# Dense products of a two-sequence encoder layer: token parts of 512 and 272 (256) columns in place of two equal halves

## The chip, the cores and the metric

The kernel runs on one core of one Trainium2 chip. The metric is the device time of one execution in microseconds, and the time of a kernel is the median of its runs. TensorE (PE) multiplies, VectorE (DVE), ScalarE (ACT) and GpSimd (POOL) work on vectors, and SyncE (SP) issues the DMAs. All of them run their own instruction streams in order and meet at semaphores.

## The reference

Two sequences, of 512 and of 256 tokens with 1024 features, each get the same 16 meta tokens in front and pass through one layer. All values are float32.

```python
h = h + 0.5 * swiglu(rmsnorm(h, ffn1_norm_w), ffn1_w_gate, ffn1_w_up, ffn1_w_down)   # width 2816
u = rmsnorm(h, mix_norm_w)
q, k, v, z, xbc, dt_raw = split(u @ w_in)                                            # 1024 -> 5408
att = diff_attention(q, k, v, rel_bias, ...)            # 8 heads, two softmaxes each
ssm = ssd_mixer(z, xbc, dt_raw, ...)                    # convolution, state space both ways, gate, norm
h = h + concatenate([att, ssm]) @ w_out                 # 2048 -> 1024
h = h + 0.5 * swiglu(rmsnorm(h, ffn2_norm_w), ffn2_w_gate, ffn2_w_up, ffn2_w_down)
return rmsnorm(h, final_norm_w)[:, 16:]
```

The meta tokens are the same for both sequences, so up to the mixer they are computed once.

## The kernel before

Features lie on the 128 partitions and tokens along the columns. The first feed-forward and the input projection work on T1 = 784 columns (16 meta, 512, 256), the output projection and the second feed-forward on T2 = 768. A dense product (`dense`, `mm3`) takes each float32 operand as a large part and a rest, and makes three matmuls for each 128 rows of the inner dimension: L246, L247 and L248, with a weight block of 128 x 128 as the stationary and a range of token columns as the moving operand. One unit is all the matmuls of one 128-row output block over one part of the tokens: 24 for an inner dimension of 1024, 12 or 6 in the products that are done in pieces (`down`, `o_unit`). A unit goes to one bank of PSUM (`ps_mm` and `ps_x`, two buffers each, 512 columns wide), and one VectorE or ScalarE operation takes it from there.

The parts of the tokens are in two lists: HALF1 (two times 392 of T1) and HALF2 (two times 384 of T2). REAL is HALF2 moved by the 16 meta columns, for the products z and q. HALF1 is used by the first feed-forward, by `x_unit` (the state-space mixer's input), `dt_unit` and `k_units` (keys). HALF2 is used by `o_unit` (output projection) and the second feed-forward. Two places have other parts: the first feed-forward's first gate and up products take PARTS (272, 256, 256), and the second's last down product takes LAST (512, 256).

`ffn` goes through pairs of feature blocks, gate then up, and adds the down product up in six groups. In the last group it goes over all eight output blocks for the first part of the tokens, then over all for the second. `Norm.after` follows it there: for each output block it squares the sum on ScalarE (L294) and adds the squares up on GpSimd (L295), with VectorE for the last block (L298). When the eighth block of a part is done, `Norm.chain` is put on the agenda: `tok_rstd` sums the squares by token on TensorE (L306) and takes 1/sqrt in a dozen small VectorE operations, `diags` and `bcast` (L275, L283, L285) spread it over the partitions, and `make_u` makes the eight normed row blocks, each with L317 on VectorE, L147 on ScalarE and L148 on VectorE. A column of `tok_rstd` holds the token count `tn`: 98 for HALF1, 128 for HALF2. `done`, called after each unit, takes the next weights apart (L147, L148 on 1024 columns) and moves each entry of the agenda one step on. So the norm of the first part goes on beside the products of the second. The same class stands between the output projection and the second feed-forward, there behind the last of the four parts of `o_unit`.

Beside the input projection the state-space mixer goes on as a row of side steps, some for each unit (PACE). Beside attention, units of k, v and the output projection are handed out by the list FILL, a number for each tile of queries. The order on each engine is that of the program with small shifts by the framework's planner, which orders by its own estimates.

Of the kernel before, what the change touches and what calls it, by code (L numbers as in the profile page):

```python
# [47 lines left out]
def body(tc, x_prompt, x_sample, meta_tokens, ffn1_norm_w, ffn1_w_gate, ffn1_w_up, ffn1_w_down,  # L48
# [48 lines left out]
    # Silu's table, before the first data are there  # L97
# [3 lines left out]
    HALF1 = [(0, T1 // 2), (T1 // 2, T1 // 2)]  # L101
    HALF2 = [(0, T2 // 2), (T2 // 2, T2 // 2)]
# [47 lines left out]
    @contextmanager  # L150
    def behind(ins):
        """Keep the engines' order: first ins, then what is in the block."""
        with ExitStack() as st:
            for i in ins:
                st.enter_context(tc.issue_after(i.ins))
            yield
# [66 lines left out]
    def done(free=0):  # L223
        """A dense product has been issued: the next weights, then a step of what goes on beside it."""
# [6 lines left out]
    def complete(gen):  # L231
        """All of gen is issued by now."""
        if gen in agenda:
            agenda.remove(gen)
            for _ in gen:
                pass
# [21 lines left out]
    def rsqrt(v, name):  # L258
        """1/sqrt of a small tile of positive numbers: a first guess from the bits, then Newton's steps."""
# [11 lines left out]
    def diags(r, tiles):  # L271
        """diag(r[:n, j]) for each of tiles (j, n)."""
# [5 lines left out]
    def bcast(dst, dg, tiles):  # L278
        """dst's columns get the diagonals of dg, the same on each partition."""
# [7 lines left out]
    def add_sq(h, m, sums):  # L287
        """The squares of row m; the last row's are added to the others' sum by tok_rstd."""
# [11 lines left out]
    def tok_rstd(sums, n, tn, name):  # L300
        """sums of [P, n]: squares by feature row; 1/rms per token, tn tokens to a column."""
# [10 lines left out]
    def make_u(h, w, r_bc, c0, c1, u, ks):  # L312
        """u = the normed rows, columns c0..c1, split; r_bc starts at c0."""
# [9 lines left out]
    class Norm:  # L323
        """Follows the last additions to h, one half of the tokens at a time."""

        def __init__(self, h, w, halves, tn, name):
            self.__dict__.update(h=h, w=w, halves=halves, tn=tn, name=name)
# [4 lines left out]
        def after(self, m, hf):  # L332
            o, n = self.halves[hf]
            add_sq(self.h[m][:, o:o + n], m, self.ss.setdefault(hf, []))
            if m == KD - 1:
                self.chains[hf] = self.chain(o, n, self.ss[hf])
                later(self.chains[hf])

        def get(self, hf):
            """The split rows, good for a half (or, without one, whole)."""  # L340
# [4 lines left out]
        def chain(self, o, n, ss):  # L345
# [3 lines left out]
            tiles = [(j, self.tn) for j in range(n // self.tn)]  # L349
            r = tok_rstd(ss, n, self.tn, self.name)  # L350
# [9 lines left out]
    def ffn(f, h, halves, u, after, first=None, last=None, rms=None):  # L360
        """first, last: other parts of the tokens for the first gates and the last sums; rms: 1/rms, if u is without."""
# [106 lines left out]
    # the first norm's 1/rms, which the products with the gates get afterwards  # L468
# [9 lines left out]
    def put_h(eng, j, ps, c, n):  # L478
        """One engine to a tile of PSUM."""
# [8 lines left out]
    def squares(tiles):  # L488
        """Sums of squares by token; the squares themselves go nowhere."""
# [8 lines left out]
    def first_norm(tiles, ss):  # L498
        """1/rms of some of the tokens."""
# [9 lines left out]
    def take_x(b, ins):  # L509
        """Two tiles of tokens; ins: what their work on each engine stays behind."""  # L510
# [25 lines left out]
    # the first two tiles one by one, the meta tokens with the first  # L536
# [59 lines left out]
    def parameters():  # L596
# [31 lines left out]
        # the relative bias as a function of the distance, one row per head  # L628
# [22 lines left out]
    nm = Norm(h1, mixw, HALF1, 98, "nm")  # L651
# [32 lines left out]
    HT = T1 // 2  # L684
# [3 lines left out]
    def dt_unit(ws):  # L688
        """Both parts of w against the large part of u, side by side; they are added up in the transposes."""
# [12 lines left out]
    def x_unit(ws, t, hf, free):  # L702
# [12 lines left out]
        else:  # L715
            S.copy(pad[:, 3 + HT:3 + HT + E0], ps[:, :E0])
            S.copy(pad[:, SO + 3 + NMETA:SO + 3 + NMETA + NSA], ps[:, E0:HT])
# [656 lines left out]
```

## Time and profile before

| | us |
|---|---|
| median of 3 runs | 1912.74 |
| lowest, highest | 1911.93, 1917.85 |
| span of the profiled execution, first to last instruction | 1908.7 |
| TensorE busy | 1865.3 (98%) |
| VectorE busy | 1012.4 (53%) |
| ScalarE busy | 699.2 (37%) |
| GpSimd busy | 97.0 (5%) |

The profiled execution's own time stands in the profile only as its span; what a timed run has above a span (start and end) is in the runs' figures alone. A matmul's printed duration contains the way through the array, which overlaps with the next one, so the time that a matmul takes from TensorE's stream is the distance between two starts. The granted clock (PEclk) is a share of full speed, 1.00 being 2.4 GHz and 0.50 being 1.2 GHz.

### The profile page before, as it was taken

The page shows a single profiled execution, that of the slowest core. Times are in us where ns is not written, and L with a number is a line of the kernel's source. Part 1 is how long each engine was busy: PE and PEld are TensorE (multiplying, and loading weights), DVE is VectorE, ACT ScalarE, POOL GpSimd, SP SyncE. Part 2 cuts the span into 40 slices and gives each one's busy share as a digit, 9 for nine tenths or more (in the row PEclk, how much of TensorE's full clock was granted, in tenths as well). Part 3 has the DMA queues.
Part 4 walks back from the last instruction along what each step waited for, and adds up shares of the span by engine and source line. Part 5 has one row for each costly group of instructions (what it writes and reads, how often), then busy time and mean ns, then how long its engine had stood idle before and what let it go on. Part 6 is the DMA issues. An engine that isn't in the chain of part 4 may idle for free.

```text
span 1908.7 us, 27592 instructions
## 1 busy us (share of the span) xinstructions
PE 1865.3 (98%) x11174; PEld 1798.8 (94%) x11174; DVE 1012.4 (53%) x2025; ACT 699.2 (37%) x1410; POOL 97.0 (5%) x118
## 2 busy tenths in 40 slices
PE   8999999999999999999899999999999999999998
PEld 7999999999998997888898998999999999999997
DVE  6444343344437498667788787666542424232333
ACT  6222121212123353678467675433322121222224
POOL 0000000000012000224100000002000000000002
PEclk9999999999998999999999999999899999999999
DMA  4242221222112232888432225321121212122111
GB/s 136 61 165 69 65 66 46 66 67 67 57 54 92 69 85 77 228 219 210 147 94 83 73 82 195 104 78 45 56 78 59 63 56 77 56 67 67 58 53 67
DMA packets 161266, 169.77 MB, mean 89 GB/s; under 512 B 9921, under 2 KB 146234, under 8 KB 161138
## 3 DMA queue, kind: packets, MB, share of 16 engines
q1 hardware_dynamic: 161122, 168.00, 28.7%
q8 instruction: 88, 1.44, 0.3%
q14 instruction: 40, 0.33, 0.1%
q10 hardware_dynamic: 16, 0.00, 0.0%
HBM read 148.54 MB, written 22.87 MB: 90 GB/s over the span
## 4 chain that ended last, share of the span: by engine, by line
PE 86%; DVE 7%; ACT 3%; DMA 1%; issue 1%; POOL 0%; SPq 0%; POOLq 0%; DVEq 0%; ACTq 0%
PE ps_mm L248 15%; PE ps_mm L247 15%; PE ps_mm L246 15%; PE ps_x L246 11%; PE ps_x L248 11%; PE ps_x L247 11%; DVE w L726 2%; PE ps_s L1162 2%; PE ps_s L1280 1%; DMA w<-ar_d 1%; ACT w L909 1%; DVE wl L148 1%; PE ps_s L841 1%; DVE w L1072 1%; DVE w L1182 1%
## 5 line engine op out<-in xcount | busy, mean ns | idle before, releaser
L248 PE MATMUL ps_mm<-rowu,wh 128*128 128x384 f32 (+3 forms) x1408 | 477.1, 339 | 4.8 <-DVE rowu L148 4.6
L246 PE MATMUL ps_mm<-rowu,wh 128*128 128x384 f32 (+3 forms) x1408 | 476.7, 339 | 4.6 <-DVE w L1041 2.0
L247 PE MATMUL ps_mm<-rowu,wl 128*128 128x384 f32 (+3 forms) x1408 | 475.9, 338 | 1.0 <-DVE wl L148 1.0
L148 DVE TENSOR_TENSOR wl<-wr,wh 128x1024 fp32r<-128x1024 f32 (+1 forms) x194 | 234.4, 1209 | 258.2 <-ACT wh L147 257.8
L147 ACT CAST wh<-wr 128x1024 fp32r<-128x1024 f32 (+1 forms) x194 | 198.4, 1024 | 391.0 <-PE ps_x L248 358.0
L247 PE MATMUL ps_x<-rowu,wl 128*128 128x392 f32 (+3 forms) x832 | 282.0, 339 | 0.0
L246 PE MATMUL ps_x<-rowu,wh 128*128 128x392 f32 (+3 forms) x832 | 281.9, 339 | 0.0
L248 PE MATMUL ps_x<-rowu,wh 128*128 128x392 f32 (+3 forms) x832 | 281.8, 339 | 0.0
L246 PEld LDWEIGHTS ps_mm<-rowu,wh 128*128 128x128 f32 x1408 | 266.0, 189 | 10.1 <-issue 2.7
L248 PEld LDWEIGHTS ps_mm<-rowu,wh 128*128 128x128 f32 x1408 | 265.6, 189 | 8.8 <-DVE rowu L148 6.4
L247 PEld LDWEIGHTS ps_mm<-rowu,wl 128*128 128x128 f32 x1408 | 265.9, 189 | 3.1 <-issue 1.4
L246 PEld LDWEIGHTS ps_x<-rowu,wh 128*128 128x128 f32 x832 | 158.5, 190 | 0.1
L247 PEld LDWEIGHTS ps_x<-rowu,wl 128*128 128x128 f32 x832 | 158.4, 190 | 0.0
L248 PEld LDWEIGHTS ps_x<-rowu,wh 128*128 128x128 f32 x832 | 158.1, 190 | 0.0
L147 ACT CAST w<-w 128x384 fp32r<-128x384 f32 (+4 forms) x106 | 59.0, 557 | 231.6 <-DVE w L390 228.5
L246 PE MATMUL ps_x<-w,wh 128*128 128x392 f32 (+3 forms) x352 | 119.7, 340 | 0.0
L246 PE MATMUL ps_mm<-w,wh 128*128 128x392 f32 (+3 forms) x352 | 119.5, 339 | 0.0
L248 PE MATMUL ps_mm<-w,wh 128*128 128x392 f32 (+3 forms) x352 | 119.4, 339 | 0.0
L248 PE MATMUL ps_x<-w,wh 128*128 128x392 f32 (+3 forms) x352 | 119.3, 339 | 0.0
L247 PE MATMUL ps_x<-w,wl 128*128 128x392 f32 (+3 forms) x352 | 119.0, 338 | 0.0
L247 PE MATMUL ps_mm<-w,wl 128*128 128x392 f32 (+3 forms) x352 | 118.8, 338 | 0.0
L410 DVE SCALAR_TENSOR_TENSOR w<-ps_x,w 128x392 f32<-128x392 f32 (+3 forms) x96 | 53.8, 561 | 113.1 <-PE ps_x L248 113.1
(286 smaller groups left out, 2587.8 us busy)
## 6 DMA issues: line engine op xcount, KB each, us to landing
wr<-in_ffn_w_gate_dram SPq DMA_DIRECT2D x44, 512.0 KB
wr<-in_ffn_w_up_dram SPq DMA_DIRECT2D x42, 512.0 KB
wr<-in_w_in_dram SPq DMA_DIRECT2D x42, 512.0 KB
wr<-in_ffn_w_down_dram SPq DMA_DIRECT2D x40, 512.0 KB
w<-ar_d SPq DMA_DIRECT2D x24, 512.0 KB
wr<-in_w_out_dram SPq DMA_DIRECT2D x16, 512.0 KB
w<-ar_d SPq DMA_DIRECT2D x24, 256.0 KB
w<-q_d SPq DMA_DIRECT2D x32, 192.0 KB
```

The lines of the kernel that those rows point to most:

```text
L147: a = S.copy(hi, src)
L148: return a, V.tensor_tensor(lo, src, hi.bitcast(F32), ALU.subtract)
L246: nc.tensor.matmul(ps, ah, bh, start=start, stop=False)
L247: nc.tensor.matmul(ps, al, bh, start=False, stop=False)
L248: last_mm[0] = nc.tensor.matmul(ps, ah, bl, start=False, stop=stop)
L410: V.scalar_tensor_tensor(dst, ps[:, :n], 0.5, dst, ALU.mult, ALU.add)
L726: V.scalar_tensor_tensor(acc, pad[:, j:j + XW], prmT[:, cw:cw + 1], acc, ALU.mult, ALU.add)
L841: nc.tensor.matmul(ps[64 * d:64 * d + 64, g, :], B[:n, 64 * g:64 * g + 64], xd[:n, g * 512:(g + 1) * 512], start=True, stop=True)
L909: S.activation(ab[d][:, h, :], ab[d][:, h, :], AF.Exp, bias=ssm["asp"][:, c, col_s:col_s + 1])
L1072: V.tensor_tensor(dst[b], ps[a, s0:s1], dst[a].bitcast(F32), ALU.subtract)
L1162: nc.tensor.matmul(ps[:, b, :w], qh[c][part][:, P * i:P * i + P], kh[c][:, k0 + b * w:k0 + b * w + w], start=part == 0, stop=part == 1)
L1182: V.tensor_tensor_reduce(out=e[:, :nk].rearrange("p (b w) -> p b w", b=nb), in0=pss[c][:, :nb, :w], in1=tb[:, x0:x0 + nk].rearrange("p (b ...
```

## The change

HALF1 becomes 512 and 272 columns, HALF2 (and with it REAL) 512 and 256. The norm's token count per column becomes one for each part: 128 and 68 for HALF1 (four columns each), 128 and 128 for HALF2 (four columns and two). The small tiles of `tok_rstd` get a name of their own for each part. In `x_unit` the boundary between the two sequences, at column 528, falls 16 columns into the second part, so the copies of the first part are of 512 and 16 columns and those of the second of 16 and 256. The comments are taken out.

```diff
-    HALF1 = [(0, T1 // 2), (T1 // 2, T1 // 2)]
-    HALF2 = [(0, T2 // 2), (T2 // 2, T2 // 2)]
+    HALF1 = [(0, 512), (512, T1 - 512)]
+    HALF2 = [(0, 512), (512, T2 - 512)]
...
-        def __init__(self, h, w, halves, tn, name):
-            self.__dict__.update(h=h, w=w, halves=halves, tn=tn, name=name)
+        def __init__(self, h, w, halves, tns, name):
+            self.__dict__.update(h=h, w=w, halves=halves, tns=tns, name=name)
...
-                self.chains[hf] = self.chain(o, n, self.ss[hf])
+                self.chains[hf] = self.chain(o, n, self.tns[hf], self.ss[hf])
...
-        def chain(self, o, n, ss):
+        def chain(self, o, n, tn, ss):
...
-            tiles = [(j, self.tn) for j in range(n // self.tn)]
-            r = tok_rstd(ss, n, self.tn, self.name)
+            tiles = [(j, tn) for j in range(n // tn)]
+            r = tok_rstd(ss, n, tn, self.name + str(o))
...
-    nm = Norm(h1, mixw, HALF1, 98, "nm")
+    nm = Norm(h1, mixw, HALF1, (128, 68), "nm")
...
-    HT = T1 // 2
+    HT = 512
...
-            S.copy(pad[:, SO + 3 + NMETA:SO + 3 + NMETA + NSA], ps[:, E0:HT])
+            S.copy(pad[:, SO + 3 + NMETA:SO + 3 + NMETA + NSA], ps[:, E0:n])
...
-    nf = Norm([None] * KD, n2w, HALF2, P, "nf")
+    nf = Norm([None] * KD, n2w, HALF2, (P, P), "nf")
```

## Rows read from the trace of the kernel before

**Rows 1.** The page's head and its first part: busy us, share, instructions.

```profile
span 1908.7 us, 27592 instructions
PE 1865.3 (98%) x11174; PEld 1798.8 (94%) x11174; DVE 1012.4 (53%) x2025; ACT 699.2 (37%) x1410; POOL 97.0 (5%) x118
```

**Rows 2.** Who waited for whom, TensorE, whole span: us, times, longest.

```profile
PE ps_x L922 <- DVE w L914: 5.4, 6, 2.2
PE ps_mm L248 <- DVE rowu L148: 4.6, 4, 1.7
PE ps_x L306 <- POOL w L295: 3.0, 2, 2.5
```

**Rows 3.** Stretches: us, PE, PEld, DVE, ACT, POOL busy (count), PEclk, DMA.

```profile
572.10:591.70 19.60, 19.60 (x121) 19.31 (x121) 16.68 (x37) 8.50 (x15) 5.63 (x4) 1.00 0.39 135
591.70:600.30 8.60, 4.73 (x26) 4.14 (x24) 8.60 (x11) 3.85 (x9) 4.06 (x4) 0.98 0.48 173
600.30:611.50 11.20, 11.18 (x49) 11.13 (x49) 3.16 (x17) 0.56 (x2) 1.89 (x17) 0.56 0.08 21
...
1312.50:1331.50 19.00, 18.98 (x117) 18.70 (x116) 16.20 (x36) 7.86 (x13) 5.38 (x4) 1.00 0.19 56
1331.50:1339.90 8.40, 5.70 (x26) 4.58 (x26) 8.40 (x11) 3.70 (x8) 3.34 (x3) 0.84 0.20 64
1339.90:1349.50 9.60, 9.60 (x43) 9.60 (x42) 3.16 (x16) 2.15 (x3) 0.00 (x0) 0.60 0.19 56
...
1000.00:1100.00 100.00, 98.38 (x672) 90.08 (x670) 82.19 (x269) 69.36 (x195) 0.00 (x0) 1.00 0.24 74
```

**Rows 4.** Groups by form, TensorE, L248: count | busy us, mean ns.

```profile
L248 PE MATMUL ps_mm<-rowu,wh 128*128 128x384 f32 x832 | 282.9, 340 | 3.4 <-DVE rowu L148 3.2
...
L248 PE MATMUL ps_mm<-rowu,wh 128*128 128x392 f32 x528 | 179.6, 340 | 1.4 <-DVE rowu L148 1.4
...
L248 PE MATMUL ps_mm<-w,wh 128*128 128x392 f32 x176 | 60.0, 341 | 0.0
...
L248 PE MATMUL ps_x<-w,wh 128*128 128x384 f32 x144 | 48.6, 337 | 0.0
```

**Rows 5.** Instructions in order of time, TensorE, starts of units: start us, us.

```profile
24.70 0.29 PE L246 MATMUL ps_mm<-rowu,wh 128*128 128x272 f32 x1
...
30.73 0.28 PE L246 MATMUL ps_mm<-rowu,wh 128*128 128x256 f32 x1
...
323.67 0.34 PE L246 MATMUL ps_mm<-rowu,wh 128*128 128x392 f32 x1
...
332.24 0.34 PE L246 MATMUL ps_mm<-rowu,wh 128*128 128x392 f32 x1
...
1353.77 0.33 PE L246 MATMUL ps_x<-rowu,wh 128*128 128x384 f32 x1
...
1362.09 0.33 PE L246 MATMUL ps_x<-rowu,wh 128*128 128x384 f32 x1
...
1864.72 0.39 PE L246 MATMUL ps_mm<-w,wh 128*128 128x512 f32 x1
...
1881.20 0.28 PE L246 MATMUL ps_mm<-w,wh 128*128 128x256 f32 x1
...
1884.05 0.28 PE L246 MATMUL ps_mm<-w,wh 128*128 128x256 f32 x1
```

**Rows 6.** Groups by form, VectorE and GpSimd, at 392, 512 and 256 columns.

```profile
L410 DVE SCALAR_TENSOR_TENSOR w<-ps_x,w 128x392 f32<-128x392 f32 x48 | 27.1, 565 | 54.3 <-PE ps_x L248 54.3
...
L410 DVE SCALAR_TENSOR_TENSOR w<-ps_x,w 128x512 f32<-128x512 f32 x4 | 2.8, 692 | 7.8 <-PE ps_x L248 7.8
...
L410 DVE SCALAR_TENSOR_TENSOR w<-ps_x,w 128x256 f32<-128x256 f32 x4 | 1.7, 425 | 3.9 <-PE ps_x L248 3.9
...
L295 POOL TENSOR_TENSOR w<-w,w 128x392 f32<-128x392 f32 x12 | 15.4, 1284 | 64.5 <-ACT w L294 64.5
...
L295 POOL TENSOR_TENSOR w<-w,w 128x256 f32<-128x256 f32 x6 | 4.4, 734 | 12.6 <-ACT w L294 12.6
```

## The prediction

> **What bounds the kernel now.** I read the page's head first. TensorE is busy for 1865.3 of 1908.7 us [rows 1], so a reader should look for two things: what one matmul costs in TensorE's own stream, and the few places where TensorE waits. The waits of TensorE [rows 2] are short, and two kinds matter here. One is for rows of the normed input (L148, written by VectorE) and for the sums of squares (L295 on GpSimd, ahead of L306). The other is the state-space mixer's (L922). The stretches [rows 3] show where the first kind lies: at the two boundaries at which a norm stands between two dense products. I call them the first (about 572 to 611 us, into the mixer) and the second (about 1312 to 1350 us, into the second feed-forward).
>
> At the first, the stretch 591.7 to 600.3 us keeps TensorE busy for 4.73 us, with 26 instructions where 48 such matmuls have room. VectorE is busy for all of its 8.60 us, so VectorE ends it. The stretch behind it runs at a granted clock of 0.56, about the lower level (1.2 GHz) against the higher (2.4 GHz). At the second, 1331.5 to 1339.9 us is the same picture, with 8.40 of 8.40 us of VectorE, and 0.60 behind it.
>
> **Part 1, the matmuls.** Nothing is removed: the dense products have the same number of matmuls and columns, in pairs of 512 and 272 where there were 392 and 392, and of 512 and 256 where there were 384 twice. The price of one is the distance between starts, not the printed duration, since matmuls overlap. Starts [rows 5] lie 24 matmuls apart per unit in the feed-forwards' gate products and 12 in the last down products:
> - 392 columns: 332.24 - 323.67 = 8.57 us for 48 (one unit of each half), 178.5 ns each.
> - 384: 1362.09 - 1353.77 = 8.32 us for 48, 173.3 ns.
> - 512: 1881.20 - 1864.72 = 16.48 us for 72, 228.9 ns.
> - 256: 1884.05 - 1881.20 = 2.85 us for 24, 118.75 ns.
> - 272: 30.73 - 24.70 = 6.03 us for 48, 125.6 ns.
>
> So a pair of 392 goes from 357.0 to 228.9 + 125.6 = 354.5 ns (-2.5), and a pair of 384 from 346.7 to 228.9 + 118.75 = 347.65 ns (+1.0). The four groups of L248 with 392 columns hold 528 + 400 + 176 + 176 = 1280 matmuls, and those with 384 hold 832 + 384 + 144 + 144 = 1504 (the first and the last of each four stand in [rows 4]). L246 and L247 have as many, so there are 1280 x 3 / 2 = 1920 pairs and 1504 x 3 / 2 = 2256 pairs. That is 1920 x -2.5 ns = -4.8 us and 2256 x +1.0 ns = +2.2 us, together -2.6 us. A nanosecond of error per pair is 4.2 us over all 4176 pairs, so the ends are -7 and +2 us.
>
> Here a rule can be weighed. The rows give a matmul more than a fixed time per column: 392 columns are dearer than half of 272 + 512 [rows 5]. The Trainium skill (TensorE: Matmul & The Clock Gate, "Back-to-back issue gap") puts the warm gap at N / 2.4 + 2.5 ns, by which equal counts and equal columns cost equally, and this part would be 0 instead of -2.6 us. The measured spacings exceed that rule by some 10 to 13 ns each, so the rows decide.
>
> **Part 2, the boundaries.** The first part of the tokens ends in the last down product; its norm (the chain: L306, the small VectorE operations of `rsqrt`, `diags`, `bcast`, then eight times L317 and L148 on VectorE with L147 on ScalarE) runs while TensorE works on the second part. The next product then needs these rows. Two things change. The cover shrinks, since the second part is smaller. The chain grows, since the first part is larger.
>
> TensorE's work from the end of the first part (572.1) to where it is let go (600.3, L306 of the second part) is 8 units of 12 matmuls and one of 24. By the spacings above that is 8 x 12 x 178.5 ns + 24 x 178.5 ns = 17.1 + 4.3 = 21.4 us. After the change it is 8 x 12 x 125.6 + 24 x 228.9 ns = 12.1 + 5.5 = 17.6 us: 3.8 us less. At the second boundary (1312.5 to 1339.9) it is 16.6 + 4.2 = 20.8 us, and after 11.4 + 5.5 = 16.9 us: 3.9 us less. These columns are not gone; they lie outside the stretch now. If VectorE ends the stretch when it does today, the kernel gets longer by 3.8 + 3.9 = 7.7 us.
>
> Does VectorE end it sooner or later? Between its two ends VectorE is busy for 16.68 + 8.60 of 28.2 us, and 16.20 + 8.40 of 27.4 us [rows 3], so the answer is its work. Sixteen row operations go from 392 to 512 columns: 692 - 565 = 127 ns each by the L410 rows [rows 6], +2.0 us. Eight evictions go from 392 to 272, about (565 - 425) x 120 / 136 = 124 ns less each, -1.0 us. GpSimd's sums, next to which VectorE's operations are slow, shrink from 1284 ns to about 734 [rows 6]; some five of them fall into the stretch, which gives back 0 to 2 us. The four weight splits in it are the same, but the buffers come free sooner, and one split more may be taken ahead of the last rows (1024 columns, at most two times 692 ns, 1.4 us). The chain starts about 0.6 us earlier, since L306 stands behind one unit of 272 instead of 392 columns (2.1 to 1.5 us). All this is -1.6 to +2 us for each boundary; I take -0.6. So the two cost 7.7 - 1.2 = +6.5 us, with ends of 4 and 12.
>
> The norm of the second part is smaller and has more cover: three units of 24 x 228.9 ns = 5.5 us instead of 4.3 stand before its rows are needed. No wait is seen there today, so nothing is won.
>
> **Part 3, everything beside it.** Evictions, splits and squares keep their number and their total columns, so VectorE, ScalarE and GpSimd have the same sum. In `x_unit` and `k_units` the 136-column piece becomes 16, and 392 becomes 512. No DMA is added or moved in order; SP's queue and GpSimd's order stay. What changes is that units alternate between about 5.5 and 3.0 us instead of 4.2 each, while the mixer's side steps and the softmax tiles are handed out by the unit. Cover today: at 1000 to 1100 us VectorE is busy for 82.19 of 100 us and TensorE still for 98.38 [rows 3]. A side step behind a short unit loses 1.3 us of cover, one behind a long unit gains as much. The waits of L922 for L914 total 5.4 us in six [rows 2]; were all to fall on short units it is 6 x 1.3 = +8 us, all on long ones -5.4. I take 0, nearest to the mean of alternating units, and ends of -3 and +5.
>
> **Sum.** -2.6 + 6.5 + 0 = +3.9 us. The profiled execution has a span of 1908.7 us, 4.0 below the median of the runs, 1912.74, which I take as what lies around it and leave as it is: 1912.6 for the span, 1916.6 us for the median.
>
> **The rivals.**
> - Slower: the clock. After each boundary TensorE runs at 0.56 and 0.60. That is 11.2 x (1 - 0.56) = 4.9 us and 9.6 x (1 - 0.60) = 3.8 us of full clock lost [rows 3]. My sum keeps these. TensorE's empty time ahead of them grows from about 5 to 9 us each. If the lower clock comes earlier and stays for as much longer as the gap has grown, another 2 to 4 us are lost at each: 1920 to 1925 us. For: both falls of the clock stand right behind such a gap. Against: while TensorE waits for rows, a lower clock costs nothing. It decides once the low stretch outlasts the wait by more than it does today. Uneven cover in the mixer and attention (up to +5) lands in the same place. Chance 0.26.
> - Faster: VectorE's chain shortens by as much as the cover. GpSimd's shorter sums and the end of the wait for L295 (2.5 us of the stretch at the first boundary, [rows 2]) return 2 to 3 us at each, and part 1 has its better end, -5: 1912.74 - 5 + 2 = 1909 to 1910, and 1906 if part 3 also gives. Chance 0.19.
> - Columns alone set a matmul's spacing, beside an equal time for each: then pairs with the same sum of columns cost the same, part 1 is 0, and the kernel takes 1912.74 + 6.5 = 1919.2 us. Five spacings that don't lie on one line [rows 5] speak against it. This is what the Trainium skill's formula, named above, would make of it. Chance 0.05.
>
> **How the numbers follow.** The forecast case has 0.50, from 1913 to 1920. About 0.3% (5.7 us) is what a measurement of this kernel can tell from no change: below 1907.0 is faster, above 1918.5 slower. Of the 0.50 some 0.07 lie above 1918.5, of the slower rival's 0.26 some 0.23, and 0.04 of the 0.05 of columns alone; of the faster rival's 0.19 some 0.10 lie below 1907.0. So faster 0.10, same 0.56, slower 0.34. The range of 8 in 10 takes in most of both rivals: 1907 to 1925.
>
> **What would show it.** A spacing of 512 and 272 columns in the first feed-forward that sums to 354 to 355 ns shows part 1. The two stretches at the boundaries, cut at the same events, should be as long as now (28.2 and 27.4 us, give or take 2), with VectorE busy throughout and TensorE 3.8 us emptier. The clock behind them tells the slower rival. The prediction is wrong if VectorE does not end these stretches, if 512 columns cost more beside the feed-forward's evictions than in the last product, or if the mixer's waits change by more than 5 us.

## The result, and the profile after

The changed kernel takes 1923.41 us (median of 5 runs, 1920.82 to 1928.37) against 1912.74 us: a ratio of 1.0056 with a 95% interval of 1.0040 to 1.0072, so 10.7 us slower. That is inside the predicted range (1907 to 1925), 6.8 us above the forecast, and past the 0.3% that the forecast took as no change. Three of the experiments below had one slow run each, of 2455 us or more; their medians and ratios are of the other runs.

The page's head and first part of the changed kernel, as in [rows 1]:

```profile
span 1926.7 us, 27599 instructions
PE 1874.7 (97%) x11174; PEld 1621.9 (84%) x11174; DVE 1010.2 (52%) x2025; ACT 699.9 (36%) x1410; POOL 95.7 (5%) x118
```

The profiled run is the slowest of its five: 1928.37 us for a span of 1926.7, so 1.7 us lie around a span. By that, the profiled run of before took 1908.7 + 1.7 = 1910.4 us, 2.3 below its median. The two traces are therefore 18.0 us apart where the medians are 10.7. The prediction took the whole 4.0 us between span and median for what lies around the span; 2.3 of them were that run's luck.

TensorE is busy for 9.4 us more with the same 11174 instructions. In the rest of the 18.0 us TensorE is idle. To place both I cut each trace at the same matmuls: the second pair of gates, the last down group, the x products, dt, the first and the last scores, the last quarter of the output projection, the second feed-forward's first gates, its second pair and its last group. A "passage" is the last down group and the x products, or the last quarter of the output projection and the first gates. "Again" is a second trace of the changed program (below, pace by columns).

| us | before | after | again | long first at the norms | small first at the norms | small first everywhere | the same, second body equal |
|---|---|---|---|---|---|---|---|
| first body | 497.4 | 497.4 | 497.4 | 497.4 | 497.4 | 497.2 | 497.2 |
| first passage | 82.4 | 79.9 | 79.9 | 80.1 | 74.0 | 75.5 | 74.1 |
| mixer | 317.1 | 329.2 | 325.2 | 317.6 | 322.7 | 318.6 | 322.2 |
| attention | 303.5 | 306.5 | 307.0 | 303.5 | 305.1 | 305.6 | 305.8 |
| second passage | 79.0 | 82.6 | 82.5 | 83.2 | 74.2 | 73.9 | 72.5 |
| second body | 484.4 | 487.2 | 487.2 | 484.5 | 484.5 | 487.2 | 484.3 |
| all else | 145.0 | 143.9 | 143.6 | 144.8 | 144.3 | 144.1 | 143.8 |

The 18.0 us are -2.5 in the first passage, +12.1 in the mixer, +3.0 in attention, +3.6 in the second passage, +2.8 in the second feed-forward's body and -1.0 elsewhere. In the second trace they are 14.1, with +8.1 in the mixer and the other lines the same within 0.5.

The stretches of [rows 3] in the changed kernel, cut at the same events (end of the first part's products, first wait for normed rows, L306 of the second part), and the stretch beside attention; columns as there:

```profile
576.30:593.35 17.05, 16.10 (x124) 15.33 (x123) 13.81 (x33) 7.23 (x12) 3.82 (x4) 1.00 0.40 144
593.35:604.50 11.15, 7.79 (x29) 4.50 (x27) 10.49 (x16) 5.16 (x10) 4.84 (x5) 1.00 0.46 151
604.50:614.00 9.50, 9.49 (x57) 8.05 (x58) 3.86 (x19) 1.71 (x5) 1.90 (x17) 1.00 0.09 25
1329.80:1346.50 16.70, 15.76 (x126) 14.98 (x125) 13.57 (x32) 7.18 (x12) 3.65 (x4) 1.00 0.11 33
1346.50:1357.50 11.00, 7.67 (x25) 3.92 (x23) 10.38 (x16) 6.36 (x10) 5.41 (x4) 0.92 0.28 81
1357.50:1367.00 9.50, 9.48 (x28) 7.85 (x29) 2.43 (x14) 0.01 (x1) 0.00 (x0) 0.56 0.25 75
1000.00:1100.00 100.00, 98.73 (x686) 87.61 (x687) 81.88 (x265) 68.98 (x194) 0.00 (x0) 1.00 0.25 74
```

From 576.30 to 604.50 are 28.2 us, from 1329.80 to 1357.50 are 27.7: as long as in [rows 3] (28.2 and 27.4). The stretch from the first wait for rows to L306 has grown, from 8.60 and 8.40 to 11.15 and 11.00 us, with VectorE busy for 10.49 and 10.38 of it. TensorE is not idle all that time: it was busy for 4.73 and 5.70 us of it, now for 7.79 and 7.67. Behind the second boundary the clock is 0.56, as it was 0.60. Behind the first it is 1.00 where it was 0.56.

TensorE's waits in the changed kernel, the rows that answer [rows 2] and those that have grown (us, times, longest):

```profile
PE ps_x L922 <- DVE w L914: 10.9, 7, 3.6
PE ps_mm L248 <- DVE rowu L148: 4.9, 9, 0.9
PE ps_s L1162 <- DVE nmx L1182: 3.3, 7, 0.9
PE ps_s L819 <- ACT w L730: 3.0, 2, 2.5
...
PE ps_x L306 <- POOL w L295: 2.0, 3, 0.8
```

L922's wait for L914 has doubled; how much of that is a new wait stands under part 3 below. L819 (transposes of convolved tiles, whose last step is the Silu of L730) is new.

Starts of TensorE's units in the changed kernel, in the first and in the second feed-forward (start us, us), as in [rows 5]:

```profile
322.57 0.40 PE L246 MATMUL ps_mm<-rowu,wh 128*128 128x512 f32 x1
...
328.12 0.29 PE L246 MATMUL ps_x<-rowu,wh 128*128 128x272 f32 x1
...
331.16 0.40 PE L246 MATMUL ps_mm<-rowu,wh 128*128 128x512 f32 x1
...
1440.28 0.39 PE L246 MATMUL ps_mm<-rowu,wh 128*128 128x512 f32 x1
...
1445.83 0.28 PE L246 MATMUL ps_x<-rowu,wh 128*128 128x256 f32 x1
...
1448.67 0.40 PE L246 MATMUL ps_mm<-rowu,wh 128*128 128x512 f32 x1
```

With 24 matmuls to a unit, 512 columns take 5.55 / 24 = 231.3 ns in both places, not 228.9. 272 take 3.04 / 24 = 126.7 and 256 take 2.84 / 24 = 118.3. A pair is 358 ns where 392 twice was 357.0, and 349.6 ns where 384 twice was 346.7.

### The profile page after: what moved, and what is told of

Its sections match the earlier page's. It is cut to its first block, busy times and chain, and to the rows that moved or that the text cites. A ratio compares the mean times of both kernels' runs of the same rounds, so it can differ in the third digit from the quotient of the medians.

```text
span 1926.7 us, 27599 instructions
## 1 busy us (share of the span) xinstructions
PE 1874.7 (97%) x11174; PEld 1621.9 (84%) x11174; DVE 1010.2 (52%) x2025; ACT 699.9 (36%) x1410; POOL 95.7 (5%) x118
## 4 chain that ended last, share of the span: by engine, by line
PE 85%; DVE 10%; ACT 2%; issue 2%; DMA 2%; POOL 0%; SPq 0%; DVEq 0%; POOLq 0%; ACTq 0%
PE ps_mm L247 17%; PE ps_mm L248 17%; PE ps_mm L246 17%; PE ps_x L246 8%; PE ps_x L248 8%; PE ps_x L247 8%; DVE w L726 2%; PE ps_s L1162 2%; PE ps_s L1280 1%; DVE wl L148 1%; DMA w<-ar_d 1%; PE ps_s L841 1%; DVE w L1072 1%; PE ps_x L922 1%; DVE w L317 1%
## 5 line engine op out<-in xcount | busy, mean ns | idle before, releaser
L246 PE MATMUL ps_mm<-rowu,wh 128*128 128x512 f32 (+2 forms) x1408 | 519.4, 369 | 6.9 <-DVE w L1120 2.0
L248 PE MATMUL ps_mm<-rowu,wh 128*128 128x512 f32 (+2 forms) x1408 | 516.1, 367 | 4.9 <-DVE rowu L148 4.9
L247 PE MATMUL ps_mm<-rowu,wl 128*128 128x512 f32 (+2 forms) x1408 | 516.9, 367 | 1.0 <-DVE wl L148 1.0
L248 PEld LDWEIGHTS ps_mm<-rowu,wh 128*128 128x128 f32 x1408 | 266.5, 189 | 55.2 <-DVE rowu L148 9.3
L246 PE MATMUL ps_x<-rowu,wh 128*128 128x272 f32 (+2 forms) x832 | 245.1, 295 | 0.4 <-DVE w L1120 0.4
L247 PE MATMUL ps_x<-rowu,wl 128*128 128x272 f32 (+2 forms) x832 | 244.8, 294 | 0.0
L248 PE MATMUL ps_x<-rowu,wh 128*128 128x272 f32 (+2 forms) x832 | 243.4, 293 | 0.0
L248 PEld LDWEIGHTS ps_x<-rowu,wh 128*128 128x128 f32 x832 | 158.3, 190 | 2.2
L147 ACT CAST w<-w 128x512 fp32r<-128x512 f32 (+3 forms) x106 | 59.1, 558 | 269.4 <-DVE w L390 264.4
L246 PE MATMUL ps_mm<-w,wh 128*128 128x512 f32 (+2 forms) x352 | 135.1, 384 | 0.4 <-DVE w L410 0.4
L247 PE MATMUL ps_mm<-w,wl 128*128 128x512 f32 (+2 forms) x352 | 135.0, 383 | 0.0
L248 PE MATMUL ps_mm<-w,wh 128*128 128x512 f32 (+2 forms) x352 | 134.9, 383 | 0.0
L410 DVE SCALAR_TENSOR_TENSOR w<-ps_mm,w 128x512 f32<-128x512 f32 (+2 forms) x96 | 64.3, 669 | 100.5 <-PE ps_mm L248 99.5
L246 PE MATMUL ps_x<-w,wh 128*128 128x272 f32 (+2 forms) x352 | 104.1, 296 | 0.6 <-DVE w L410 0.6
L247 PE MATMUL ps_x<-w,wl 128*128 128x272 f32 (+2 forms) x352 | 104.1, 296 | 0.0
```

The lines of the kernel that those rows point to most:

```text
L147: a = S.copy(hi, src)
L246: nc.tensor.matmul(ps, ah, bh, start=start, stop=False)
L247: nc.tensor.matmul(ps, al, bh, start=False, stop=False)
L248: last_mm[0] = nc.tensor.matmul(ps, ah, bl, start=False, stop=stop)
L410: V.scalar_tensor_tensor(dst, ps[:, :n], 0.5, dst, ALU.mult, ALU.add)
```

## The experiments

All ratios are against the kernel before, measured again beside each experiment (medians 1912.4 to 1914.4 us), with 95% intervals. "Equal parts" means 392 + 392 or 384 + 384. The short diffs show the lines that matter, against the changed kernel unless said otherwise.

**Only the parts of 784 columns** (first feed-forward, x, dt, k; first norm).

```diff
-    HALF2 = [(0, 512), (512, T2 - 512)]
+    HALF2 = [(0, T2 // 2), (T2 // 2, T2 // 2)]
```

> Only HALF1 is 512 and 272 (first feed-forward, first boundary, x, dt and k products); HALF2 and z, q stay in equal parts. Theory A (the time sits where cover became uneven or small: the boundaries and the side steps of the mixer): +3 to +6 us against the kernel before, of which the first boundary has +2 to +3 without the clock and x units in the mixer the rest. Theory B (the time sits in the matmuls: 512 columns cost 231 ns beside the gate products and not 228.9): the pairs of this kernel cost 231.1 + 126.7 = 357.8 against 357.2 ns, so +0 to +1 us.

Measured: 1915.42 us, 1.0014 (1.0005 to 1.0023). First body 497.4, first passage 79.9, mixer 322.5, attention 306.1, second passage 79.3, second body 484.4. So the first body is indifferent, attention's +2.6 belongs to these parts, and the second half of the kernel is as before.

**Only the parts of the output projection and the second feed-forward** (second norm).

```diff
-    HALF1 = [(0, 512), (512, T1 - 512)]
+    HALF1 = [(0, T1 // 2), (T1 // 2, T1 // 2)]
-    REAL = [(NMETA + o, n) for o, n in HALF2]
+    REAL = [(NMETA, T2 // 2), (NMETA + T2 // 2, T2 // 2)]
```

> Only the output projection and the second feed-forward are in parts of 512 and 256; HALF1 and the z and q products stay equal. Theory A: the second boundary costs +3 to +4 us, the second feed-forward nothing: +3 to +4. Theory B: besides, the 1056 gate and up pairs of the second feed-forward cost 231.7 + 118.5 = 350.2 against 346.7 ns, 1056 x 3.5 ns = +3.7 us, less 0.5 to 1 in the down products: together with the boundary +6 to +7 us.

Measured: 1919.26 us, 1.0030 (1.0019 to 1.0040). Second passage 82.6 against 79.0, second body 487.2 against 484.4, attention 303.9. The second boundary and the second body are +3.6 and +2.8 by themselves, as in the whole change.

**Only z and q of the mixer** in 512 + 256.

```diff
-    HALF1 = [(0, 512), (512, T1 - 512)]
-    HALF2 = [(0, 512), (512, T2 - 512)]
-    REAL = [(NMETA + o, n) for o, n in HALF2]
+    HALF1 = [(0, T1 // 2), (T1 // 2, T1 // 2)]
+    HALF2 = [(0, T2 // 2), (T2 // 2, T2 // 2)]
+    REAL = [(NMETA, 512), (NMETA + 512, T2 - 512)]
```

> Only the z and q products (32 units in the mixer) are in parts of 512 and 256, all else as before. If the mixer's added waits come from side steps that follow a short unit: +3 to +6 us. If they come from the time at which the mixer's inputs arrive (x products) or from the order of the engines elsewhere: 0 to +1 us, of which 384 pairs x 1.6 ns = 0.6 us are the matmuls.

Measured: 1917.60 us, 1.0023 (1.0013 to 1.0032). The mixer takes 323.9 us, all else is as before. TensorE's mixer waits in this trace:

```profile
PE ps_x L922 <- DVE w L914: 9.2, 7, 3.7
PE ps_s L819 <- ACT w L730: 2.5, 1, 2.5
```

The new wait of L819 comes with these parts alone. The three edits by themselves, this one and the two above, cost 2.7, 5.7 and 4.4 us by their ratios, 12.8 together, against 10.7 for the whole change; with intervals of some 2 us to each side for each, that is the same sum.

**Pace by columns.** The mixer's side steps were to follow the columns of each product.

```diff
-        acc[0] += PACE[kind]
+        acc[0] += PACE[kind] * share
```

> The changed kernel, but in the mixer the side steps are handed out by columns (2.61 and 1.39 steps behind units of 512 and 272 columns, 2.67 and 1.33 behind 512 and 256) and not two by the unit. If uneven cover makes the mixer's added waits, 3 to 6 of the some 7 us come back: 1917 to 1920 us. If the waits have another cause, no change against the changed kernel: 1922 to 1925 us.

This edit changed nothing: 2 x 512 x 2 / 784 = 2.6 steps round to two, the remainder and the short product's 1.4 to two again, and the instructions are the changed kernel's. It serves as a second measurement of that program: 1927.45 us, 1.0081 (1.0066 to 1.0097), mixer 325.2 us. So two groups of runs of one program are 0.25% apart, about as much as the single edits above cost by their totals; the times of their stages say more. The same two rows of waits (columns as above):

```profile
PE ps_x L922 <- DVE w L914: 10.8, 8, 3.6
PE ps_s L819 <- ACT w L730: 3.0, 2, 2.5
```

**Steps three and one, and one and three.** The dealing for real: three side steps behind each long product and one behind each short one, then the reverse.

```diff
-    def steps(kind):
-        acc[0] += PACE[kind]
+    def steps(kind, extra=0):
+        acc[0] += PACE[kind] + extra
...
-                    steps(kind)
+                    steps(kind, (1, -1)[hf])
```

> The changed kernel with the mixer's side work dealt out by columns: three steps behind each product of 512 columns, one behind each of 272 or 256, instead of two and two. The number of steps is the same. Theory (uneven cover): the short products with two steps leave TensorE waiting for VectorE, so the mixer's +6.4 to +7.0 at equal clock falls to about +2 (what the z and q columns cost, +0.6, and a rest), total 1918 to 1919 us. Rival (the order of the side work is indifferent, the waits come from the long chains themselves): mixer unchanged within 2 us, total 1923 to 1927. Second rival (three steps in a row pile up ahead of VectorE's eviction of the product): mixer longer by 2 us or more.

Measured: 1925.42 us, 1.0059 (1.0042 to 1.0076), mixer 326.1.

> The changed kernel with the mixer's side work dealt out against the columns: one step behind each product of 512, three behind each of 272 or 256. Theory (uneven cover): TensorE's idle time beside the mixer, 56 to 57 us in the two traces of the changed kernel and 54.6 with three and one, grows by 4 us or more, total 1927 to 1931. Rival (the idle time hangs on where the long chains fall, not on the dealing): within 2 us of the changed kernel, 1923 to 1927.

Measured: 1922.90 us, 1.0050 (1.0037 to 1.0064), mixer 327.8. The mixer's waits, three-and-one first:

```profile
PE ps_x L922 <- DVE w L914: 10.0, 6, 3.6
PE ps_s L819 <- ACT w L730: 3.9, 2, 2.0
```

```profile
PE ps_x L922 <- DVE w L914: 12.7, 7, 4.7
PE ps_s L819 <- ACT w L730: 5.8, 3, 4.9
```

The waits move by a few microseconds as the theory of uneven cover would have it (13.9 against 18.5 us in these two rows), but the mixer stays within 325 to 329 us and the total doesn't follow. How the steps are dealt to long and short products does not account for the mixer's loss in these traces.

**Only the passages at the norms.** Equal parts everywhere but in the last down group, the x products, the last quarter of the output projection and the first gates.

```diff
+    EDGE1 = [(0, 512), (512, T1 - 512)]
+    EDGE2 = [(0, 512), (512, T2 - 512)]
-    ffn(1, h1, HALF1, u_first, nm.after, first=PARTS, rms=rms1)
+    ffn(1, h1, HALF1, u_first, nm.after, first=PARTS, rms=rms1, last=EDGE1)
-    ffn(2, h2l, HALF2, nf.get, final, last=LAST)
+    ffn(2, h2l, HALF2, nf.get, final, last=LAST, first=EDGE2)
```

> 512 + 272 (or 256) columns only in the passages before and behind each norm: the last sums and x products around the first norm, the last quarter of the output projection and the first gates around the second. Every other dense product keeps equal halves. Theory (the passages lose cover, whatever the clock does): last group of the first feed-forward +2.2, x products up to dt +0.4, output projection's last quarter +2.7, first gates +0.9, together +6.2 us at equal clock; the bodies of both feed-forwards and the mixer's z and q 0. Without a clock fall at the first norm 5.1 us come back, so 1913.5 us, or 1918.6 with it. Rival 1 (the loss comes from the columns of all products, the passages are only where it shows): under +1.5 at equal clock. Rival 2 (the second norm's loss belongs to the long products before it): last quarter of the output projection under +1.

Measured: 1914.75 us, 1.0005 (0.9990 to 1.0019). Passages 80.1 and 83.2, all else as before. The second passage is +4.2, also without long products ahead of it. The first is -2.3, and the reason is the clock: the x products up to dt, before, here, and with the small part first (columns as in [rows 3]):

```profile
591.70:637.40 45.70, 41.80 (x219) 41.13 (x218) 22.09 (x49) 13.08 (x33) 5.95 (x20) 0.89 0.19 61
```

```profile
593.90:634.90 41.00, 37.60 (x218) 31.42 (x217) 21.21 (x54) 13.56 (x34) 7.12 (x21) 1.00 0.25 77
```

```profile
591.00:630.20 39.20, 38.94 (x218) 34.19 (x217) 19.55 (x43) 12.17 (x28) 5.69 (x19) 0.96 0.18 55
```

A mean clock of 0.89 over 45.70 us is at most 5.0 us lost. Without them the first passage of before would take no less than 77.4 us, so at equal clock the long part first costs up to 2.5 us there (79.9 against 77.4 in the changed kernel).

**The passages with the small part first.**

```diff
-    EDGE1 = [(0, 512), (512, T1 - 512)]
-    EDGE2 = [(0, 512), (512, T2 - 512)]
+    EDGE1 = [(0, 272), (272, T1 - 272)]
+    EDGE2 = [(0, 256), (256, T2 - 256)]
-    nm = Norm(h1, mixw, EDGE1, (128, 68), "nm")
+    nm = Norm(h1, mixw, EDGE1, (68, 128), "nm")
```

> As the run with 512 + 272 (256) in the passages alone, but with the small part first: 272 + 512 and 256 + 512. Theory (cover): the products on the second part hide the first part's chain, and are now longer than before, so what the passages lose on the first part goes (about -3.8 each against equal halves). The second part's chain grows: 16 make_u steps, each 692 - 565 = 127 ns longer, +2.0, and the product that hides its start is 24 x 54 ns = 1.3 us shorter. About -0.5 us each, 1911 to 1914 us, so 4 to 7 us under the run with the long part first at equal clock. Rival (only the sizes count, not the order): the same +6.2 at equal clock as with the long part first. Second rival (VectorE's whole work at a norm sets the end, order and sizes both indifferent): 0.

Measured: 1901.94 us, 0.9931 (0.9907 to 0.9955). Passages 74.0 and 74.2 us: 6.1 and 9.0 under the long part first. At the first norm neither kernel has a fall of the clock; at the second the long part first has one of 10.2 us and this one of 3.4, which at half the clock is at most 3.4 us of the 9.0. What is left, 6.1 and at least 5.6, is more than the 4 to 7 us expected for both together, and the sizes are the same, so the order is the cause. I had charged the longer chain of the second part with 2.0 us at each norm. No such cost shows: the program issues four units of the first part (24 matmuls of 272 columns each, 12 us) before the first unit that needs the second part's rows.

**The whole change with the small part first.**

```diff
-    HALF1 = [(0, 512), (512, T1 - 512)]
-    HALF2 = [(0, 512), (512, T2 - 512)]
+    HALF1 = [(0, 272), (272, T1 - 272)]
+    HALF2 = [(0, 256), (256, T2 - 256)]
```

> The whole change with the small part first: 272 + 512 and 256 + 512 in every dense product and in both norms, all else as in the changed kernel. Theory (the passages lose because the short second part covers too little of the long first part's chain; the columns cost what they cost in any order): the last group of the first feed-forward 36.3 instead of 38.9 us, x products up to dt 37.7 instead of 41.0, last quarter of the output projection 35.9 instead of 38.6, first gates 38.9 instead of 44.0, together -13 to -14 us against the changed kernel (some 4 of it a clock fall that goes with the wait); the body of the second feed-forward keeps its +2.8, the mixer its +5 to +8 beyond the kernel before. Total 1908 to 1912 us. Rival 1 (the order is indifferent, the uneven parts themselves cost): 1922 to 1926. Rival 2 (512 columns cost more because they stand first in a pair): the second feed-forward's body falls back by 2.8 as well, 1905 to 1909.

Measured: 1903.68 us, 0.9950 (0.9935 to 0.9965). The same sizes in the other order are about 20 us faster than the changed kernel. The stretches at the two norms, cut as above:

```profile
566.80:590.98 24.18, 24.18 (x123) 19.92 (x121) 20.86 (x43) 10.18 (x18) 6.84 (x6) 1.00 0.39 135
590.98:594.42 3.44, 3.18 (x25) 2.96 (x24) 3.03 (x5) 1.80 (x3) 3.12 (x3) 1.00 0.72 257
594.42:604.00 9.58, 9.58 (x66) 9.58 (x67) 5.26 (x20) 1.86 (x6) 2.59 (x17) 0.82 0.09 24
...
1303.20:1326.70 23.50, 23.50 (x110) 19.44 (x109) 19.94 (x39) 9.48 (x17) 8.92 (x6) 1.00 0.17 48
1326.70:1329.93 3.23, 3.14 (x25) 2.91 (x24) 3.07 (x6) 1.82 (x4) 1.30 (x1) 1.00 0.47 151
1329.93:1340.00 10.07, 9.97 (x73) 9.89 (x73) 6.22 (x21) 3.74 (x6) 0.00 (x0) 0.83 0.20 55
```

The first stretch is 27.6 us, about as long as ever (28.2), but TensorE is busy for 24.18 + 3.18 of it, and VectorE is idle for 3.7. The second body keeps its 487.2 us, so 512 + 256 columns cost more there in either order. The mixer is at 318.6.

**Only the second feed-forward's body** in 512 + 256, far from any norm.

```diff
-            parts = (first or halves) if pr == 0 else halves
+            parts = (first or halves) if pr == 0 else (mid or halves)
...
+    ffn(2, h2l, HALF2, nf.get, final, last=LAST, mid=LAST)
```

> 512 + 256 columns only in the second feed-forward between its first gates and its last group, equal parts everywhere else: the columns by themselves, with no norm near. Prediction's step (512 at 228.9 ns, 256 at 118.75: one pair 1.0 ns over two of 384; with 1488 pairs +1.5 us): the body 484.4 to 486 us. What the runs so far show (231.7 + 118.5 = 350.1 against 346.7 ns behind the normed rows, 231.1 + 118.6 = 349.7 against 350.9 behind the gates' products): 487.2 us, +2.8. Elsewhere 0 in both. Total 1914 or 1915.5; the time of the body decides.

Measured: 1914.55 us, 1.0005 (0.9995 to 1.0014); the total can't tell 1.5 from 2.8 us, but the body takes 487.2 against 484.4. Two units of it:

```profile
1445.11 0.39 PE L246 MATMUL ps_mm<-rowu,wh 128*128 128x512 f32 x1
...
1450.66 0.28 PE L246 MATMUL ps_x<-rowu,wh 128*128 128x256 f32 x1
...
1453.50 0.40 PE L246 MATMUL ps_mm<-rowu,wh 128*128 128x512 f32 x1
```

5.55 us for 24 again, 231.3 ns: the price comes with these columns in these products, with no norm and no mixer near.

**400 + 384 instead of 392 + 392** in the parts of 784, all else equal.

```diff
-    HALF1 = [(0, 512), (512, T1 - 512)]
+    HALF1 = [(0, 400), (400, T1 - 400)]
-    HALF2 = [(0, 512), (512, T2 - 512)]
+    HALF2 = [(0, T2 // 2), (T2 // 2, T2 // 2)]
```

> First feed-forward, x and dt in 400 + 384 columns (norm tiles 100 and 96), all behind it in equal halves. Theory of the start (392 columns from column 392 on took 179.9 ns a matmul, the first 392 only 177.3, and 384 from column 384 on 173.3): with the second part at column 400, a multiple of 16, the pair takes 180.5 + 173.3 = 353.8 instead of 357.2 ns; times 1920 pairs, -6.5 us, 1906 us. The passage at the norm stays within 1 us, as the cover changes by 8 columns. Rival 1 (the columns alone set the spacing, any sum of 784 takes 357): 0, 1912.5. Rival 2 (what counts is the width of the tile read, not where it starts): 400 at 181 to 184, 384 at 176: -0 to +4.

Measured: 1911.93 us, 0.9996 (0.9982 to 1.0009). The units of the first feed-forward:

```profile
323.15 0.34 PE L246 MATMUL ps_mm<-rowu,wh 128*128 128x400 f32 x1
...
327.50 0.34 PE L246 MATMUL ps_x<-rowu,wh 128*128 128x384 f32 x1
...
331.69 0.34 PE L246 MATMUL ps_mm<-rowu,wh 128*128 128x400 f32 x1
```

The pair takes 8.54 / 24 = 355.8 ns, between the theory's 353.8 and the rival's 357; the first body gains 1.25 us, not 6.5. That the start column sets the price is not shown. What makes 384 columns 174.6 ns here and 173.3 in the second feed-forward stays open.

**The small part first, and the second body in equal parts** (the diff is against the small part first everywhere).

```diff
-    ffn(2, h2l, HALF2, nf.get, final, last=LAST)
+    ffn(2, h2l, HALF2, nf.get, final, last=LAST, mid=[(0, T2 // 2), (T2 // 2, T2 // 2)])
```

> The whole change with the small part first, but the second feed-forward between its first gates and its last group in equal parts of 384, where uneven parts cost 2.8 us in each run. Theory (costs add up): the body back from 487.2 to 484.4 us, the passages at the norms as with the small part first throughout (36.3, 37.7 to 39.2, 35.2, 38.6 to 38.9 us), total 1901 us. Rival (the body's 2.8 us come back elsewhere, or the seams between equal and uneven parts cost as much): 1903 to 1905.

Measured: 1902.34 us, 0.9947 (0.9933 to 0.9962). The body is back at 484.3 as added up, but the total can't be told from the 1903.68 and 1901.94 us of the two kernels with the small part first. All three beat both the kernel before and the changed one. Against the kernel before, a part of that can be the clock: over all runs, the span times one less its mean granted clock, which is the most that the lower clock can have cost, is 21.5 us there and 12.9 to 14.9 in these three.

## Why the prediction was right and wrong

**Right in its range, wrong in its likeliest case.** The forecast gave no measurable change 0.56 and slower 0.34. Two of its three terms missed, in the same direction, and a clock that went the other way hid some of it; that the range held is in part luck.

**Part 1, the matmuls: the sign was wrong.** The failed step is the price of 512 columns: a spacing read in one product was used for all. It was read over six units of the last down product [rows 5], at 228.9 ns; in the gate products of the change it is 231.3, and 272 columns take 126.7 for 125.6. The prediction named this as what would undo it, but gave the term -2.6. A spacing that sums to 354 to 355 ns was to show this part right; it sums to 358. Measured: 0.0 in the first body and +2.8 in the second, the latter also alone. Over all gate and up products, and over all down products, of a body (start of the first matmul to start of the next product, divided by the pairs), one pair takes:

| ns per pair | pairs | before | after | forecast of the change |
|---|---|---|---|---|
| first body, gate and up | 960 | 357.2 | 357.8 | -2.5 |
| first body, down | 432 | 356.7 | 355.8 | -2.5 |
| second body, gate and up | 960 | 346.7 | 350.1 | +1.0 |
| second body, down | 432 | 350.9 | 349.7 | +1.0 |

The down products, where the price was read, did get cheaper; the gate and up products, more than two thirds of the pairs, did not. The rows add up to the bodies' 0.0 and +2.8 within 0.2 us. The rival that columns alone set the spacing falls all the same: in the second body's gate products equal columns cost 346.7 and 350.1 ns.

What sets the price is not shown. That matmuls of another width follow does not explain it: in the changed kernel's first feed-forward, last down group, eight units of 512 columns follow one another (first two rows), and take 22.18 us for 96, 231.0 ns each. The six units at 228.9 ns, which the change leaves as they are, take 16.56 us for 72 there (last two rows), 230.0 ns:

```profile
554.11 0.39 PE L246 MATMUL ps_mm<-w,wh 128*128 128x512 f32 x1
...
576.29 0.29 PE L246 MATMUL ps_mm<-w,wh 128*128 128x272 f32 x1
...
1882.66 0.39 PE L246 MATMUL ps_mm<-w,wh 128*128 128x512 f32 x1
...
1899.22 0.27 PE L246 MATMUL ps_mm<-w,wh 128*128 128x256 f32 x1
```

**Part 2, the boundaries: right in kind, at most 6 of the 6.5 us.** That the stretch stays as long although TensorE has less to do in it is shown by 28.2 and 27.7 us. VectorE is not busy throughout, as the prediction asked: it is for 10.49 of the last 11.15 us, and the profile puts the last 0.8 us down to a sum on GpSimd, behind VectorE's last work (L306 waits for L295). TensorE's loss of cover is smaller than forecast: in the two stretches 30 and 28 matmuls of 512 columns start where the forecast counted 24, since the planner took some of a later unit ahead. By the prediction's spacings TensorE has 18.9 us of matmuls for 21.4 (2.5 less, not 3.8) and 17.8 for 20.8 (3.0, not 3.9). The term was +6.5; measured are up to +2.5 at the first norm and +3.6 at the second, at most some 6 together. The prediction's remark that three units of 24 x 228.9 ns are 5.5 us, for the second part's cover, gives one unit; three are 16.5 us. Inside the stretch, the sums on GpSimd did not shrink to 734 ns as [rows 6] suggested. L295 in the changed kernel, then with the small part first everywhere (GpSimd, by form: count | busy us, mean ns):

```profile
L295 POOL TENSOR_TENSOR w<-w,w 128x256 f32<-128x256 f32 x12 | 13.2, 1104 | 31.2 <-ACT w L294 31.2
L295 POOL TENSOR_TENSOR w<-w,w 128x272 f32<-128x272 f32 x6 | 8.4, 1394 | 19.5 <-ACT w L294 19.5
```

```profile
L295 POOL TENSOR_TENSOR w<-w,w 128x256 f32<-128x256 f32 x12 | 8.8, 735 | 386.9 <-ACT w L294 386.9
L295 POOL TENSOR_TENSOR w<-w,w 128x272 f32<-128x272 f32 x6 | 4.6, 772 | 42.9 <-ACT w L294 42.9
```

The 272 columns take 1394 ns where they are the second part and fall beside VectorE's chain, and 772 where they are the first part and don't. The 1284 ns of [rows 6] for 392 columns are a mean of both: 1.02 to 1.03 us for each of the six sums of the first part, and 1.07 to 2.28 us, 1.54 in the mean, for the six of the second. So in their own place the sums fell from 1.54 to 1.39 us; the forecast's 734 ns is a price without that neighbour. This also took from the faster rival what it counted on.

**The clock.** The slower rival expected longer falls. At the second norm the fall stayed in both traces of the changed program (0.56 for 9.5 us, before 0.60 for 9.6), but it is absent with three and one steps. With the small part first everywhere the clock fell for 3.4 us behind both norms (0.82 and 0.83 in the rows above), although TensorE had been busy for 3.18 of 3.44 and 3.14 of 3.23 us. At the first it went away in the changed program, both times, and in the other kernels with 512 + 272 there but one (where it was shorter), while every kernel with equal halves has it. That gave back up to 5.0 us. The longer stretch behind the first wait did not bring a longer fall; TensorE was busy for 7.79 of its 11.15 us, before for 4.73 of 8.60. Over all runs, the span times one less its mean granted clock is 21.5 us in 79 runs of the kernel before, and 13.8 and 18.6 in the 5 and 6 runs of the changed program. Why the fall fails to come there is open. The rival's time, 1920 to 1925, held the result, but by its other mechanism.

**Part 3, everything beside it: the largest miss.** It was put at 0, with ends of -3 and +5. Measured: +8.1 and +12.1 in the mixer in two traces, and +3.0 and +3.5 in attention. That the mixer's waits change by more than 5 us was on the list of what would make the prediction wrong, and the rows of L922 for L914 and of L819 are 5.5 and 3.0 us longer. Not all of the 5.5 is a new wait, since L922 waits for others too. Before, after, and with the small part first in the passages alone (there the line is L926, and the mixer is in equal parts):

```profile
PE ps_x L922 <- DVE w L914: 5.4, 6, 2.2
PE ps_x L922 <- ACT wh L147: 3.6, 1, 3.6
PE ps_x L922 <- ACT w L909: 1.2, 1, 1.2
```

```profile
PE ps_x L922 <- DVE w L914: 10.9, 7, 3.6
PE ps_x L922 <- ACT w L909: 2.8, 1, 2.8
```

```profile
PE ps_x L926 <- DVE w L918: 11.5, 7, 3.8
```

So L922 waits for 10.2 us before, 13.7 after, and 11.5 in a kernel whose mixer has equal parts; 3.5 of the 5.5 us at most are the change's. The failed step is the bound: it counted only the waits that were there, and L819's 3.0 us had no row in the trace of before.

How sure is the size? Five traces with equal parts in the mixer gave 317.1, 317.6, 320.2, 322.2 and 322.7 us (one with 400 + 384 gave 324.5). Four with the long part first gave 325.2, 326.1, 327.8 and 329.2; with it in x, dt and k alone, or in z and q alone, it was 322.5 and 323.9. With the small part first in all of it, two gave 318.6 and 322.2. So the long part first costs the mixer some 7 us in the mean (327.1 against 320.0), and the other order nothing that these traces can tell. The trace of before, at 317.1, is the lowest of its kind, so the 8.1 and 12.1 us overstate the cost. The clock has a part in it too: inside the mixer it is at the lower level for 10.2 us in the trace of before, and for 20.5 and 13.7 in the two of the changed program. With half of that taken off everywhere, the most that it can have cost, the five traces give 312.1 us in the mean, the four 316.9 and the two 310.2, so some 5 us are left at equal clock. Attention's rise comes with the parts of 784 columns (303.5 to 306.1 alone) and is there in either order. By what path the order reaches the mixer is not settled. The wait of L819 for a convolved tile, 2.5 us or more in every kernel with z and q long first, at most 1.8 in the others and absent with the small part first, goes with it. The dealing of the steps does not.

**What was not asked.** The prediction weighed sizes and not the order. Its own account of cover, 21.4 us before and 17.6 after, would have given 8 x 12 x 228.9 + 24 x 125.6 ns = 25.0 us for 272 ahead of 512. At clock 1.00 in both, the first passage takes 79.9 us with the long part first and 74.1 with the small, and the second 78.7 (with three and one steps) and 72.5 (with the second body in equal parts).

## What to carry to other kernels

Where a step between two products follows the first part's data and is hidden by the second part's products, try the small part first: its own chain is then short and its cover long, and here the last part's chain was hidden by the next product's work on the first. A spacing, or any duration, holds for the product and the neighbours where it was read, so price a changed operation from a row of the same product, with the work beside it that it will have. A wait that has no row today still needs a bound, since a finely interleaved stage can lose as much by a new wait as by all the old ones.

## What the runs showed of the hardware

Matmuls of the same shape have different prices in different products: a pair of 384 columns takes 346.7 ns in the second feed-forward's gate products and 350.9 in its down products, 384 columns take 173.3 ns in the former and 174.6 next to 400 in the first feed-forward, and 512 columns 228.9 to 231.3. A GpSimd sum of 272 columns took 772 ns in one place and 1394 in another, beside VectorE's chain. The changed program's mixer took 329.2 us in one execution and 325.2 in another, and with the same equal parts it took from 317.1 to 322.7. A fall of TensorE's clock to 0.56 behind a norm was there after a stretch of 8.60 us in which TensorE was busy for 4.73, not after one of 11.15 us in which it was busy for 7.79, and for 3.4 us after one of 3.44 us in which it was busy for 3.18.
